# One list of weight loads across the stages of a decoder step, and modulation matmuls in groups of four

## The chip, the cores and the metric

The kernel runs on one core of a Trainium2 chip. The metric is the device time of one launch in microseconds (us), the median of several runs. A core has five engines with instruction queues of their own: TensorE (PE, with its weight loads as PEld), VectorE (DVE), ScalarE (ACT), GpSimd (POOL) and SyncE (SP), which here only issues DMA transfers. [...]

## What is computed

One inference step of a 2-layer decoder for 512 prompt tokens and 8 x 4 sample tokens (width 1024, all float32). Each layer has a mixer and a convolutional feed-forward net (FFN), both between RMS norms and modulated by shift, scale and gate, which come from a matmul of the condition `c` with `ada_w`:

```python
mod = (c_act @ w["ada_w"][l] + w["ada_b"][l])[:, None, :]
sh1, sc1, g1, sh2, sc2, g2 = jnp.split(mod, 6, axis=-1)
h = _rmsnorm(x, ng[0]) * (1 + sc1) + sh1
...
x = x + g1 * _rmsnorm(y, ng[1])
h = _rmsnorm(x, ng[2]) * (1 + sc2) + sh2
y, f_new = _conv_ffn(h, f_prev, w["ffn_w_up"][l], w["ffn_conv_w"][l], w["ffn_conv_b"][l], w["ffn_w_down"][l])
x = x + g2 * _rmsnorm(y, ng[3])
```

Mixer 0 is a gated convolution beside causal pooling, mixer 1 is dilated attention (the sample tokens against a cache) beside a convolution module. Outputs are the activations, the new convolution states and the shifted caches (`o_c`, copied from DRAM to DRAM).

## The kernel before

Tokens lie along the columns: 544 columns in two halves `h` of 272, features on the 128 partitions. A large matmul is done in three passes for accuracy: `Hhi*whi`, `Hlo*whi`, `Hhi*wlo` (lines 527, 529, 531). So every weight tile of 128 x 512 is loaded by SP into `wraw` (7 buffers), copied by ACT to the rounded `whi` (L510), and the remainder `wlo` is formed by DVE or POOL (L511); `whi` and `wlo` have 8 buffers each, which is four blocks of two tiles. A block of 128 outputs is 8 k-steps x 3 passes x 2 halves = 48 matmuls, and its result is evicted from PSUM by the stage's own function.

`gemm` (L536) runs one matmul of the model over its blocks. The first blocks of a stage (`lead`) and the last (`tail`) are done half by half, so that the norm of one half can run while TensorE works on the other; `junction` (L496: `postres`, then `premod`) is that norm. `gemm` loads a block's weights when it comes to the block; the lead's `wlo` are formed on POOL (30 tiles in all), the others on DVE. The stages are mixer 0 (`w_abi`, `w_abo`), FFN 0, mixer 1 (`w_cdi`, attention, `w_cdo`) and FFN 1.

Side work is woven in, one step after each block: `ada` (L397) for the modulation, `bias_vectors`, `caches`. One step of `ada` is four loads of 128 x 512 and four matmuls whose stationary operand has 32 columns, each to its own 32 partitions of one PSUM bank (128*32 in the profile); 8 steps make one third of a layer's modulation, then four transposes and a few DVE operations turn it to the partitions. The first of these is done at the start, before the first block, since nothing can begin without it; the five others run in mixer 0 and FFN 0.

A scheduler places the instructions on each engine's queue by its own estimate of when they can run; the order in the code is only where it starts. So the four matmuls of a step need not stand together, and a cache copy may stand far ahead of its place in the code.

Of the kernel before, what the change touches and what calls it, by code (L numbers as in the profile page):

```python
# [41 lines left out]
XRB = 6  # L42
# [225 lines left out]
def build(nc, tc, ctx, t):  # L268
# [21 lines left out]
    cst = cp.tile([P, NCST], F32, name="cst")  # L290
    cact = cp.tile([P, KB, 32], F32, name="cact")
# [97 lines left out]
    apool = []  # L389
# [7 lines left out]
    def ada(l, s):  # L397
        ps = psum1("psada")
        for k in range(KB):
            for j in range(4):  # L400
                wt = ada_tile()
                o = s * 2048 + j * 512
                SY.dma_start(wt, t["ada_w"][l, k, :, o:o + 512])
                PE.matmul(ps[32 * j:32 * j + 32, :], cact[:, k, :], wt, start=(k == 0), stop=(k == KB - 1))  # L404
            yield
        ev = np_.tile([P, 512], F32, name="adaev", tag="nsq", bufs=NSQ)
        A.activation(ev, ps, AF.Copy)
        pt = psum1("psadat")
# [42 lines left out]
    LEADE = G  # L451
# [52 lines left out]
    def load_w(ap, kc, eng):  # L504
        raw = wp.tile([P, 512], F32, name="wraw", tag="wraw", bufs=WRAW)
        hi = wp.tile([P, 512], F32R, name="whi", tag="whi", bufs=WSLOTS)
        lo = wp.tile([P, 512], F32R, name="wlo", tag="wlo", bufs=WSLOTS)
        n = kc * P
        SY.dma_start(raw[:, :n], ap.rearrange("p k n -> p (k n)"))
        A.activation(hi[:, :n], raw[:, :n], AF.Copy)  # L510
        eng.tensor_tensor(lo[:, :n], raw[:, :n], hi[:, :n], op=SUB)  # L511
        return hi, lo

    def load_block(w, n, k0, k1, eng):
        out = []
        for a in range(k0, k1, 4):
            b = min(a + 4, k1)
            hi, lo = load_w(w[n, :, a:b, :], b - a, eng[a // 4 % 2])
            out += [(hi[:, i * P:(i + 1) * P], lo[:, i * P:(i + 1) * P]) for i in range(b - a)]
        return out  # L520

    def mm(ps, wt, src, h0, h1):
        last = len(wt) - 1
        for i, (whi, wlo) in enumerate(wt):
# [5 lines left out]
            for h in range(h0, h1):  # L530
                PE.matmul(ps[:, h, :HT], wlo, xhi[:, h, :], start=False, stop=(i == last))  # L531
# [4 lines left out]
    def gemm(w, blocks, k0, k1, src, evac, lead=0, tail=0, mids=(None, None), eng=None, loaded=()):  # L536

        nb = len(blocks)

        def halves(idx, eng, mid):  # L540
            wts = dict(enumerate(loaded)) if 0 in idx else {}
            for h in range(2):
                for i in idx:
                    if h == 0 and i not in wts:
                        wts[i] = load_block(w, blocks[i], k0, k1, eng)
# [5 lines left out]
                    mm(ps, wts[i], src, h, h + 1)  # L551
                    evac(i, blocks[i], ps, h, h + 1)
# [4 lines left out]
        yield from halves(range(lead), (G, LEADE), mids[0])  # L557
# [5 lines left out]
        yield from halves(range(nb - tail, nb), (V, V), mids[1])  # L563
# [54 lines left out]
    def ffn(l, nxt, side, pre):  # L618
# [11 lines left out]
        if l == 0:  # L630
            apool.append((fp, 4))
# [42 lines left out]
        def body():  # L674
# [19 lines left out]
    def mixer0(nxt, side, pre, loaded):  # L694
# [5 lines left out]
        apool.append((st0, XRB))  # L700
# [587 lines left out]
```

## Time and profile before

| | us |
|---|---|
| median of 3 runs | 1503.35 (1501.24 to 1504.15) |
| the profiled execution | 1496.03 |
| its span | 1494.3 |
| PE busy | 1417.8 |
| DVE busy | 882.1 |
| ACT busy | 618.8 |
| POOL busy | 170.6 |

PE is busy for 95% of the span, and 88% of the chain that ended last is PE. A busy PE counts modelled ends of pipelined matmuls, so what a piece of work costs is read from the starts of the instructions around it. Of the rest of the span, most lies at the start, at the passages from one stage to the next (the junctions), in the second half of attention, and at the end.

### The profile page before, as it was taken

How to read it: one execution, taken by the hardware profiler on the slowest of the kernel's cores; microseconds unless marked ns; L12 is line 12 of the kernel's file. 1: busy time of each engine (PE TensorE's matmuls, PEld its weight loads, DVE VectorE, ACT ScalarE, POOL GpSimd, SP SyncE). 2: the span in 40 equal slices, each digit the busy share in tenths (PEclk: the TensorE clock that was granted, in tenths of full speed). 3: DMA queues.
4: the chain of work that ended last, by engine and by line, in shares of the span. 5: the costliest groups of instructions: out<-in, count | busy, mean ns of one | idle time of the engine just before them, and what ended most of it. 6: DMA issues, size and time to landing. Idle time of an engine off the chain costs nothing.

```text
span 1494.3 us, 26853 instructions
## 1 busy us (share of the span) xinstructions
PE 1417.8 (95%) x10354; PEld 1271.0 (85%) x10354; DVE 882.1 (59%) x1788; ACT 618.8 (41%) x1145; POOL 170.6 (11%) x384
## 2 busy tenths in 40 slices
PE   6899997999999999999799999999699999999995
PEld 2578897988798798899699999678599999999995
DVE  1664427753165346446859979652886456456457
ACT  2322235743244234235652442643674444244244
POOL 0210014110011001001500000000521011011011
PEclk9799998999999999999999999999899999999998
DMA  7775633325445546544236245446122332332311
GB/s 264 242 253 187 201 106 100 103 98 180 160 155 194 161 139 212 165 158 186 89 113 197 94 141 178 135 146 239 57 85 69 103 93 71 104 91 65 113 51 61
DMA packets 112633, 207.72 MB, mean 139 GB/s; under 512 B 20884, under 2 KB 33684, under 8 KB 111992
## 3 DMA queue, kind: packets, MB, share of 16 engines
q1 hardware_dynamic: 112504, 206.00, 42.5%
q8 instruction: 81, 1.33, 0.4%
q14 instruction: 48, 0.39, 0.1%
HBM read 198.63 MB, written 34.39 MB: 156 GB/s over the span
## 4 chain that ended last, share of the span: by engine, by line
PE 88%; DVE 6%; DMA 2%; ACT 2%; issue 1%; SPq 0%; POOL 0%; POOLq 0%; DVEq 0%; ACTq 0%
PE psmm L527 23%; PE psmm L531 23%; PE psmm L529 23%; PE psada L404 6%; PE psn L442 2%; PE psmh L529 2%; PE psmh L527 2%; PE psmh L531 2%; PE pso L1013 1%; PE psl L979 1%; PE psl L981 1%; DVE X L492 1%; DVE Yf L491 1%; DVE Y L491 1%; DVE Hlo L481 1%
## 5 line engine op out<-in xcount | busy, mean ns | idle before, releaser
L510 ACT ACTIVATE whi<-wraw 128x512 fp32r<-128x512 f32 (+1 forms) x404 | 239.8, 600 | 511.4 <-PE psmm L529 411.6
L527 PE MATMUL psmm<-Hhi,whi 128*128 128x272 f32 x2028 | 435.9, 291 | 1.0 <-DVE extu L750 1.0
L531 PE MATMUL psmm<-Hhi,wlo 128*128 128x272 f32 x2028 | 431.4, 289 | 0.3 <-POOL wlo L511 0.3
L529 PE MATMUL psmm<-Hlo,whi 128*128 128x272 f32 x2028 | 430.0, 288 | 0.0
L511 DVE TENSOR_TENSOR wlo<-wraw,whi 128x512 fp32r<-128x512 f32 (+1 forms) x374 | 240.8, 649 | 303.4 <-ACT whi L510 288.3
L527 PEld LDWEIGHTS psmm<-Hhi,whi 128*128 128x128 f32 x2028 | 321.4, 189 | 24.3 <-issue 12.6
L529 PEld LDWEIGHTS psmm<-Hlo,whi 128*128 128x128 f32 x2028 | 322.5, 189 | 9.0 <-issue 9.0
L531 PEld LDWEIGHTS psmm<-Hhi,wlo 128*128 128x128 f32 x2028 | 321.5, 189 | 9.9 <-issue 9.2
L527 PE MATMUL psmm<-act_hi,whi 128*128 128x272 f32 x624 | 135.5, 290 | 0.0
L531 PE MATMUL psmm<-act_hi,wlo 128*128 128x272 f32 x624 | 135.3, 289 | 0.0
L529 PE MATMUL psmm<-act_lo,whi 128*128 128x272 f32 x624 | 132.7, 288 | 0.0
L578 DVE SCALAR_TENSOR_TENSOR fz<-fext,par,fz 128x560 f32<-128x560 f32 x88 | 70.5, 801 | 74.3 <-ACT fz L577 74.2
L404 PE MATMUL psada<-adaw,cact 128*32 128x512 f32 x384 | 102.6, 628 | 8.3 <-DMA adaw<-ada_w 8.3
L527 PEld LDWEIGHTS psmm<-act_hi,whi 128*128 128x128 f32 x624 | 99.6, 188 | 11.8 <-issue 8.4
L531 PEld LDWEIGHTS psmm<-act_hi,wlo 128*128 128x128 f32 x624 | 99.6, 188 | 7.6 <-issue 7.5
L529 PEld LDWEIGHTS psmm<-act_lo,whi 128*128 128x128 f32 x624 | 99.1, 188 | 0.8 <-issue 0.8
L577 ACT ACTIVATE fz<-fext,par 128x560 f32<-128x560 f32 x88 | 75.2, 855 | 34.5 <-DVE fext L647 34.5
L874 DVE SCALAR_TENSOR_TENSOR zd<-extd,par,zd 128x512 f32<-128x512 f32 x120 | 87.0, 746 | 0.7
L569 POOL COPY fso<-fext 128x2 f32<-128x2 f32 x88 | 23.1, 263 | 530.6 <-ACT fext L646 530.6
L579 DVE SCALAR_TENSOR_TENSOR fz<-fext,par,fz 128x560 f32<-128x560 f32 x88 | 70.5, 801 | 2.7
L646 ACT ACTIVATE fext<-psmm 128x512 f32<-128x512 f32 (+1 forms) x88 | 49.7, 564 | 51.1 <-PE psmm L531 51.1
L527 PE MATMUL psmh<-Hhi,whi 128*128 128x272 f32 x148 | 48.2, 326 | 16.1 <-ACT Hhi L479 14.5
(260 smaller groups left out, 1692.9 us busy)
## 6 DMA issues: line engine op xcount, KB each, us to landing
adaw<-ada_w SPq DMA_DIRECT2D x192, 256.0 KB, 3.6
wraw<-w_up SPq DMA_DIRECT2D x176, 256.0 KB, 3.0
wraw<-w_dn SPq DMA_DIRECT2D x64, 256.0 KB, 2.8
o_c<-cache SPq DMA_DIRECT2D x8, 2040.0 KB, 10.0
wraw<-w_cdi SPq DMA_DIRECT2D x52, 256.0 KB, 4.6
wraw<-w_abi SPq DMA_DIRECT2D x32, 256.0 KB, 4.5
o_c<-cache SPq DMA_DIRECT2D x8, 1016.0 KB, 7.1
kc<-kc SPq DMA_DIRECT2D x28, 256.0 KB, 3.7
```

The lines of the kernel that those rows point to most:

```text
L404: PE.matmul(ps[32 * j:32 * j + 32, :], cact[:, k, :], wt, start=(k == 0), stop=(k == KB - 1))
L442: PE.matmul(ps, ones, a, start=(i == 0), stop=(i == n - 1))
L510: A.activation(hi[:, :n], raw[:, :n], AF.Copy)
L511: eng.tensor_tensor(lo[:, :n], raw[:, :n], hi[:, :n], op=SUB)
L527: PE.matmul(ps[:, h, :HT], whi, xhi[:, h, :], start=(i == 0), stop=False)
L529: PE.matmul(ps[:, h, :HT], whi, xlo[:, h, :], start=False, stop=False)
L531: PE.matmul(ps[:, h, :HT], wlo, xhi[:, h, :], start=False, stop=(i == last))
L577: A.activation(z[:, :n], ext[:, 2:2 + n], AF.Identity, bias=b, scale=w[:, 2:3])
L578: V.scalar_tensor_tensor(z[:, :n], ext[:, 1:1 + n], w[:, 1:2], z[:, :n], op0=M, op1=ADD)
L579: V.scalar_tensor_tensor(z[:, :n], ext[:, 0:n], w[:, 0:1], z[:, :n], op0=M, op1=ADD)
L646: A.activation(fpr(ext, 2, h0, h1), cpr(ps, h0, h1), AF.Copy)
L874: V.scalar_tensor_tensor(cpr(z), ip, dw[:, i:i + 1], cpr(z), op0=M, op1=ADD)
```

## The change

All weight loads of the launch are put in one list ahead of time (`declare`). `take` gives a block its weights, and before that issues the loads and splits of all blocks up to two ahead, across the ends of stages too; both splits are now on ACT and DVE, none on POOL. Evictions are placed behind the newest splits on ACT and on DVE (`evacuate`). `ada` loads two 128 x 512 pieces in one transfer of 512 KB and does four matmuls of 256 columns with it, placed right behind the newest block on PE, with nothing between the four; the six thirds become twelve halves of 8 steps. The turn to the partitions is two matmuls by a selection of 9 of each 32 columns in place of four transposes. Small and large output transfers (`queued`) are placed behind the newest weight load on SP, the cache copies one to every fourth block of FFN 1; those of `o_kv` and `rvd` go to ACT's queue. At the start, the norm of half 0 begins with the first half of the modulation.

```diff
     def ada_tile():
-        if apool:
-            ap, n = apool[-1]
-            return ap.tile([P, CH, HT], F32, name="adaw", bufs=n).rearrange("p a n -> p (a n)")[:, 0:512]
-        return wp.tile([P, 512], F32, name="adaw", tag="wraw", bufs=WRAW)
+        return apool[-1].tile([P, 2, 512], F32, name="adaw", bufs=ADB[len(apool) - 1])
...
+            with tc.issue_after(newest["PE"]) if "PE" in newest else nullcontext():
+                for j in range(4):
+                    PE.matmul(ps[32 * j:32 * j + 32, :], cact[:, k, :], wt[:, j // 2, 256 * (j % 2):256 * (j % 2) + 256],
+                              start=(k == 0), stop=(k == KB - 1))
...
-        for c in range(4):
-            PE.transpose(pt[:, c * P:(c + 1) * P], ev[:, c * P:(c + 1) * P], ident)
+            for c in range(2):
+                PE.matmul(pt[:, :, c, :], ev[:, c * P:c * P + P], ssel, start=True, stop=True)
...
-    def load_w(ap, kc, eng):
+    def load_w(ap):
...
-        eng.tensor_tensor(lo[:, :n], raw[:, :n], hi[:, :n], op=SUB)
...
+        newest["SP"] = SY.dma_start(raw[:, :n], ap).ins
+        newest["ACT"] = A.activation(hi[:, :n], raw[:, :n], AF.Copy).ins
+        newest["DVE"] = V.tensor_tensor(lo[:, :n], raw[:, :n], hi[:, :n], op=SUB).ins
...
+    def take():
+
+        u, i = done
+        need = max(units[u])
+        while i < len(loads) and (i <= need or i < WSLOTS or loads[i - WSLOTS][1] <= u - 2):
+            loads[i][2] = load_w(loads[i][0])
+            i += 1
+        done[:] = [u + 1, i]
+        return [x for j in units[u] for x in loads[j][2]]
+
+    def evacuate(evac, *args):
+
+        with tc.issue_after(newest["ACT"]), tc.issue_after(newest["DVE"]):
+            evac(*args)
...
-            mm(ps, load_block(w, blocks[i], k0, k1, eng or (V, V)), src, 0, 2)
-            evac(i, blocks[i], ps, 0, 2)
+            mm(ps, take(), src, 0, 2)
+            evacuate(evac, i, blocks[i], ps, 0, 2)
...
-                SY.dma_start(t[f"o_c{g}"][b:b + n].rearrange("b w n -> b (w n)").rearrange("b (q n) -> q b n", q=16),
-                             t[f"cache{g}"][b:b + n, 4:CW[g]].rearrange("b w n -> b (w n)").rearrange("b (q n) -> q b n", q=16))
+                with queued():
+                    SY.dma_start(t[f"o_c{g}"][b:b + n].rearrange("b w n -> b (w n)").rearrange("b (q n) -> q b n", q=16),
+                                 t[f"cache{g}"][b:b + n, 4:CW[g]].rearrange("b w n -> b (w n)").rearrange("b (q n) -> q b n", q=16))
...
-    pre = mixer0((0, 1), chain(delay(1), pace(chain(ada(0, 1), ada(0, 2)), 7, 8)),
-                 second, loaded)
-    pre = ffn(0, (1, 0), chain(delay(8), bias_vectors(), slow(chain(ada(1, 0), ada(1, 1), ada(1, 2)), 2)), pre)
+    pre = mixer0((0, 1), chain(delay(1), ada([(0, i, q) for i in (1, 2) for q in range(2)], 2, 0)),
+                 lambda: (xprep(1), first(1, 0, KB)))
+    pre = ffn(0, (1, 0), chain(delay(8), bias_vectors(), pace(ada([(1, i, q) for i in range(3) for q in range(2)], 1, 0), 3, 4)), pre)
     pre = mixer1((1, 1), pre)
-    ffn(1, None, caches(), pre)()
+    ffn(1, None, slow(caches(), 3), pre)()
```

On PE in FFN 0, before, where the first step of layer 1's modulation runs (`psada` is the modulation's PSUM bank, `psmm` a block's):

```order
L529 MATMUL psmm<-Hlo,whi 128x272 x2
L404 MATMUL psada<-adaw,cact 32x512 x2
L531 MATMUL psmm<-Hhi,wlo 128x272 x2
L527 MATMUL psmm<-Hhi,whi 128x272 x2
L529 MATMUL psmm<-Hlo,whi 128x272
L404 MATMUL psada<-adaw,cact 32x512
L529 MATMUL psmm<-Hlo,whi 128x272
L531 MATMUL psmm<-Hhi,wlo 128x272 x2
L527 MATMUL psmm<-Hhi,whi 128x272 x2
L529 MATMUL psmm<-Hlo,whi 128x272
L404 MATMUL psada<-adaw,cact 32x512
```

The same place after:

```order
L608 MATMUL psmm<-Hhi,whi 128x272 x2
L610 MATMUL psmm<-Hlo,whi 128x272 x2
L612 MATMUL psmm<-Hhi,wlo 128x272 x2
L431 MATMUL psada<-adaw,cact 32x256 x4
L608 MATMUL psmm<-Hhi,whi 128x272 x2
```

The step that stood in three places of a block stands in one, at the block's end. In the whole program before, `psada` stands in 84 places, 9 of them ahead of the first block; after, in 72, 5 of them ahead of it, and of the other 67, 54 hold four matmuls and 13 hold eight.

On DVE at the junction from mixer 1 to FFN 1, before (L446 to L448 end the norm's root, L491 and L492 are `postres`):

```order
L446 SCALAR_TENSOR_TENSOR nq<-nr 128x272
L596 TENSOR_TENSOR Y_10483<-psmh,Y_10483 128x272
L447 SCALAR_TENSOR_TENSOR nq<-psn,nq 128x272
L596 TENSOR_TENSOR Y_10483<-psmm,Y_10483 128x272
L448 SCALAR_TENSOR_TENSOR nr<-nq,nr 128x272
L596 TENSOR_TENSOR Y_10483<-psmh,Y_10483 128x272
L491 TENSOR_TENSOR Y_10483<-Y_10483,nr 128x2x272 x2
L492 TENSOR_TENSOR X<-X,Y_10483 128x2x272 x2
```

The same place after:

```order
L558 TENSOR_TENSOR wlo<-wraw,whi 128x512
L494 SCALAR_TENSOR_TENSOR nq<-nr 128x272
L676 TENSOR_TENSOR Y_10539<-psmm,Y_10539 128x272
L495 SCALAR_TENSOR_TENSOR nq<-psn,nq 128x272
L558 TENSOR_TENSOR wlo<-wraw,whi 128x512
L496 SCALAR_TENSOR_TENSOR nr<-nq,nr 128x272
L676 TENSOR_TENSOR Y_10539<-psmh,Y_10539 128x272
L538 TENSOR_TENSOR Y_10539<-Y_10539,nr 128x2x272 x2
L539 TENSOR_TENSOR X<-X,Y_10539 128x2x272 x2
```

The eight splits of FFN 1's lead, which stood in one row on POOL, now stand on DVE in and around this chain: three ahead of L538, three between L539 and the next root (behind L518), two around that root.

On SP, before, a cache copy stands among the weight loads of mixer 0:

```order
L509 DMA wraw<-w_abi 128x512 x4
L1207 DMA o_c<-cache 16x3968
L403 DMA adaw<-ada_w 128x512 x4
L509 DMA wraw<-w_abi 128x512 x3
L1207 DMA o_c<-cache 16x3968
```

After, all 24 stand in FFN 1:

```order
L556 DMA wraw<-w_up 128x512 x4
L1298 DMA o_c<-cache 16x16256
L556 DMA wraw<-w_up 128x512 x6
L1298 DMA o_c<-cache 32x16320
L556 DMA wraw<-w_up 128x512 x6
```

They moved from mixer 0, FFN 0 and mixer 1 into the stage that has no modulation to load.

## Rows read from the trace of the kernel before

**Rows 1.** Busy time by stretch of the span: start and end, length, busy us and instructions of PE, PEld, DVE, ACT and POOL, then TensorE's granted clock, the DMA engines' share and GB/s. The stretches are mixer 0, FFN 0, its junction to mixer 1, the second half of attention, the junction to FFN 1, and FFN 1.
```profile
60.00:228.00 168.00, 166.92 (x1203) 139.79 (x1203) 74.67 (x159) 48.46 (x86) 13.25 (x23) 1.00 0.58 188
258.00:697.00 439.00, 439.00 (x3208) 386.41 (x3207) 223.91 (x433) 169.81 (x288) 35.96 (x128) 1.00 0.47 157
697.00:757.00 60.00, 47.03 (x312) 43.34 (x311) 49.38 (x115) 39.42 (x100) 22.76 (x26) 0.94 0.38 136
950.00:1005.00 55.00, 48.99 (x357) 35.79 (x356) 34.78 (x77) 29.31 (x44) 0.00 (x0) 0.97 0.50 166
1050.00:1095.00 45.00, 30.44 (x165) 26.12 (x165) 38.65 (x83) 29.11 (x73) 18.45 (x15) 0.85 0.15 47
1095.00:1458.00 363.00, 363.00 (x2911) 362.72 (x2910) 212.11 (x401) 160.20 (x261) 43.21 (x128) 1.00 0.29 87
```

**Rows 2.** The same view with the instructions of the tile `psada` alone, from the first block to the end of the modulation: busy PE, PEld and ACT.
```profile
60.00:645.00 585.00, 79.34 (x320) 11.06 (x320) 2.97 (x5) 0.99 0.51 166
```

**Rows 3.** PE in order of time: start, length, line, result and operands, shapes, count of records (one of these float32 matmuls of the modulation leaves two records). First a step in three pieces, then a step in one.
```profile
332.47 0.29 PE L529 MATMUL psmm<-Hlo,whi 128*128 128x272 f32 x1
332.68 1.04 PE L404 MATMUL psada<-adaw,cact 128*32 128x512 f32 x2
333.66 0.40 PE L529 MATMUL psmm<-Hlo,whi 128*128 128x272 f32 x1
...
356.36 0.41 PE L531 MATMUL psmm<-Hhi,wlo 128*128 128x272 f32 x2
356.70 1.06 PE L404 MATMUL psada<-adaw,cact 128*32 128x512 f32 x8
357.69 0.52 PE L527 MATMUL psmm<-act_hi,whi 128*128 128x272 f32 x2
```

**Rows 4.** PE in order of time in mixer 1's last matmul, where the sample's attention does groups of four matmuls of the same form with 256 columns.
```profile
1024.08 0.41 PE L531 MATMUL psmm<-Hhi,wlo 128*128 128x272 f32 x2
1024.42 1.07 PE L1157 MATMUL psr<-vc,sPT 128*32 128x256 f32 x16
1025.42 0.52 PE L527 MATMUL psmm<-Hhi,whi 128*128 128x272 f32 x2
...
1026.03 0.41 PE L531 MATMUL psmm<-Hhi,wlo 128*128 128x272 f32 x2
1026.37 0.64 PE L1157 MATMUL psr<-vc,sPT 128*32 128x256 f32 x8
1026.94 0.52 PE L527 MATMUL psmm<-Hhi,whi 128*128 128x272 f32 x2
```

**Rows 5.** PE in order of time: the four transposes that turn a third of the modulation, and four float32 matmuls with 16 columns and a whole stationary operand.
```profile
417.58 0.60 PE L410 MATMUL psadat<-cst,adaev 128*128 128x128 f32 x4
417.94 0.49 PE L527 MATMUL psmm<-Hhi,whi 128*128 128x272 f32 x2
...
1035.82 0.96 PE L1168 MATMUL psys<-cst,Rm 128*128 128x16 f32 x8
1036.62 0.50 PE L527 MATMUL psmm<-Hhi,whi 128*128 128x272 f32 x2
```

**Rows 6.** The start: busy time by stretch, columns as in rows 1, then PE in order of time.
```profile
8.00:23.00 15.00, 11.19 (x35) 3.64 (x32) 0.59 (x2) 3.44 (x7) 0.00 (x0) 1.00 1.06 378
23.00:33.00 10.00, 9.28 (x38) 3.55 (x38) 4.84 (x10) 2.01 (x4) 0.00 (x0) 1.00 0.37 115
33.00:47.50 14.50, 8.25 (x22) 1.97 (x22) 2.69 (x12) 2.79 (x5) 3.60 (x7) 0.76 0.93 319
...
37.97 6.54 PE L404 MATMUL psada<-adaw,cact 128*32 128x512 f32 x16 [1.81 <-DMA adaw<-ada_w]
47.54 0.36 PE L527 MATMUL psmh<-Hhi,whi 128*128 128x272 f32 x1 [1.62 <-DVE Hhi L1238]
```

**Rows 7.** The junction from mixer 1 to FFN 1 in order of time: POOL, then DVE. The last two rows of DVE are half 1 of the same junction.
```profile
1048.95 12.24 POOL L511 TENSOR_TENSOR wlo<-wraw,whi 128x512 fp32r<-128x512 f32 x8 [11.17 <-PE psmm L531]
1053.51 3.13 DVE L491 TENSOR_TENSOR Y<-Y,nr 128x544 f32<-128x544 f32 x2
1056.57 3.49 DVE L492 TENSOR_TENSOR X<-X,Y 128x544 f32<-128x544 f32 x2
1059.98 2.42 DVE L491 TENSOR_TENSOR Y<-Y,nr 128x544 f32<-128x544 f32 x2
1081.15 1.36 DVE L491 TENSOR_TENSOR Y<-Y,nr 128x544 f32<-128x544 f32 x2
1082.43 1.35 DVE L492 TENSOR_TENSOR X<-X,Y 128x544 f32<-128x544 f32 x2
```

**Rows 8.** Groups of instructions by line and form: the `wlo` splits of whole tiles on DVE and on POOL; busy us, mean ns of one, and what ended the idle time ahead of them.
```profile
L511 DVE TENSOR_TENSOR wlo<-wraw,whi 128x512 fp32r<-128x512 f32 x318 | 217.3, 689 | 245.7 <-ACT whi L510 236.8 <-DMA wraw<-w_up 4.0 <-PE psadat L410 2.8
L511 POOL TENSOR_TENSOR wlo<-wraw,whi 128x512 fp32r<-128x512 f32 x30 | 43.9, 1482 | 82.8 <-ACT whi L510 36.2 <-DMA wraw<-w_abi 35.5 <-PE psmm L531 11.2
```

**Rows 9.** One link of the chain that ended last, in attention's second half.
```profile
988.80 4.93 DMA wraw<-w_cdo
```

**Rows 10.** DMA issues: result and source, queue, count, KB each, median us from issue to landing.
```profile
o_c<-cache SPq DMA_DIRECT2D x8, 2040.0 KB, 10.0
o_c<-cache SPq DMA_DIRECT2D x8, 1016.0 KB, 7.1
vc<-vc SPq DMA_DIRECT2D x14, 512.0 KB, 6.9
```

More of the change, by code (lines that the diff above doesn't have):

```diff
@@ L1 @@
 import numpy as np
-from contextlib import ExitStack
+from contextlib import ExitStack, nullcontext
 import concourse.bass as bass
@@ new lines, in build, with queued, last, ada @@
+    ssel = cp.tile([P, 4, NMOD], F32, name="ssel")
+    apool = [st0]
+    newest = {}
+    def queued():
+        return tc.issue_after(newest["SP"]) if newest else nullcontext()
+    def last(eng):
+        return tc.issue_after(next(i for i in reversed(nc.cur_bb.bb.instructions) if i.engine == eng.engine))
+    def ada_tile():
+        return apool[-1].tile([P, 2, 512], F32, name="adaw", bufs=ADB[len(apool) - 1])
+    def ada(halves, per, ahead):
+        todo = [(l, s, q, k) for l, s, q in halves for k in range(KB)]
+        tiles = []
+        def load():
+            if todo[len(tiles):]:
+                l, s, q, k = todo[len(tiles)]
+                tiles.append(ada_tile())
+                with queued():
+                    SY.dma_start(tiles[-1], t["ada_w"][l].rearrange("k p (s a q n) -> s q k p a n", s=3, a=2, q=2)[s, q, k])
+        for _ in range(ahead):
+            load()
+        outs = []
+        for i, (l, s, q, k) in enumerate(todo):
+            load()
+            if k == 0:
+                ps = psum1("psada")[:, 0:256]
+            wt = tiles[i]
+            with tc.issue_after(newest["PE"]) if "PE" in newest else nullcontext():
+                for j in range(4):
+                    PE.matmul(ps[32 * j:32 * j + 32, :], cact[:, k, :], wt[:, j // 2, 256 * (j % 2):256 * (j % 2) + 256],
+                              start=(k == 0), stop=(k == KB - 1))
+            if i % per == per - 1:
+                yield
+                for o in list(outs):
+                    if next(o, 0) == 0:
+                        outs.remove(o)
+            if k == KB - 1:
+                outs.append(ada_out(l, s, q, ps))
+                if ahead:
+                    for _ in outs.pop():
+                        pass
+        while outs:
+            for o in list(outs):
+                if next(o, 0) == 0:
+                    outs.remove(o)
+            yield
@@ L530, in mm, with gemm, halves @@
             for h in range(h0, h1):
-                PE.matmul(ps[:, h, :HT], wlo, xhi[:, h, :], start=False, stop=(i == last))
+                x = PE.matmul(ps[:, h, :HT], wlo, xhi[:, h, :], start=False, stop=(i == last))
+        newest["PE"] = x.ins
     def srcH(k):
         return Hhi[:, k], Hlo[:, k]
-    def gemm(w, blocks, k0, k1, src, evac, lead=0, tail=0, mids=(None, None), eng=None, loaded=()):
+    def gemm(blocks, src, evac, lead=0, tail=0, mids=(None, None)):
+        blocks = list(blocks)
         nb = len(blocks)
-        def halves(idx, eng, mid):
-            wts = dict(enumerate(loaded)) if 0 in idx else {}
+        def halves(idx, mid):
             for h in range(2):
                 for i in idx:
-                    if h == 0 and i not in wts:
-                        wts[i] = load_block(w, blocks[i], k0, k1, eng)
                     if i % 5 in (1, 3):
@@ L555, in halves @@
                     mid()
-        yield from halves(range(lead), (G, LEADE), mids[0])
+        yield from halves(range(lead), mids[0])
         for i in range(lead, nb - tail):
             ps = psum("psmm")
-            mm(ps, load_block(w, blocks[i], k0, k1, eng or (V, V)), src, 0, 2)
-            evac(i, blocks[i], ps, 0, 2)
+            mm(ps, take(), src, 0, 2)
+            evacuate(evac, i, blocks[i], ps, 0, 2)
             yield
-        yield from halves(range(nb - tail, nb), (V, V), mids[1])
+        yield from halves(range(nb - tail, nb), mids[1])
     def fill_state(ext, L, st):
@@ L682, in body @@
                 yield from up(e + 1, FGROUPS[gi + 1][1])
-            SY.dma_start(t[f"o_f{l}"], so)
-            yield from down(ng - 1)
-            apool.clear()
+            for i, _ in enumerate(down(ng - 1)):
+                if i == 3:
+                    with queued():
+                        SY.dma_start(t[f"o_f{l}"], so)
+                yield
+            del apool[1:]
         weave(body(), side)
@@ L1180, in sample @@
             yield
-        weave(gemm(t["w_cdo"], range(KB), 2, 6, lambda k: srcH(k + 2), out_evac(Y, acc, None, True, False)), sample())
-        for _ in gemm(t["w_cdo"], range(KB), 0, 2, srcH, out_evac(Y, acc, cG[1][0], False, True), tail=KB,
+        weave(gemm(range(KB), lambda k: srcH(k + 2), out_evac(Y, acc, None, True, False)), sample())
+        for _ in gemm(range(KB), srcH, out_evac(Y, acc, cG[1][0], False, True), tail=KB,
                       mids=(None, lambda: junction(0, Y, acc, nxt))):
@@ L1248, in build @@
     SY.dma_start(cst[:, :io], t["cst"][:, :io])
+    steps(a, 2)
+    xstat(0)
     steps(a, 1)
-    xprep(0, 0, KB)
-    steps(a, 1)
-    xprep(1, 0, CH * (XRB - 4))
-    loaded = [load_block(t["w_abi"], ABI[i], 0, KB, (G, G)) for i in range(PRE)]
+    xstat(1)
+    xprep(0)
+    for i in range(2):
+        loads[i][2] = load_w(loads[i][0])
+    done[1] = 2
     for _ in a:
```

186 lines of the change are left out of this document (105 added, 81 removed).

## The prediction, made before the changed kernel ran

> **What bounds the kernel now.** I read the busy time by stretch first. In FFN 0 PE is busy 439.00 us of 439, in FFN 1 363.00 of 363, in mixer 0 166.92 of 168 [rows 1]. There nothing can shorten the launch but less work on PE, and a wait put on another engine costs nothing until PE feels it. PE has idle time at the junctions (12.97 us of 60 from FFN 0 to mixer 1, 14.56 of 45 from mixer 1 to FFN 1), in attention's second half (6.01 of 55) [rows 1], and at the start, where the first block begins at 47.54 [rows 6]. So I cost the change in two ways: by PE's time in the full stretches, and by what ends last in the others.
>
> **The modulation's matmuls.** Busy shares don't price an interruption of the stream, so I take starts. A lone matmul of 512 columns: from the block's matmul ahead of it at 332.47 to the one behind it at 333.66 is 1.19 us; two neighbouring matmuls of the block stand 0.125 apart (48 of 363.00 us over 2911 records, [rows 1]), so the interruption costs 1.07. Four of them together: from 356.36 to 357.69 is 1.33, and the two records ahead account for 0.25, which leaves 1.08 [rows 3]. An interruption costs the same whether it holds one matmul or four. Counted by the order, 75 interruptions lie behind the first block, 75 x 1.07 = 80.3; the busy time of the tile gives 79.34 [rows 2], so the count is sound.
>
> After, there are 67: 54 of four and 13 of eight, all with 256 columns. The trace has this very form, in the sample's attention: 32 columns of stationary operand and 256 moving columns. Eight records (four matmuls, as in the step of [rows 3]) cost 1026.94 - 1026.03 - 0.25 = 0.66, sixteen cost 1025.42 - 1024.08 - 0.25 = 1.09 [rows 4]. So 54 x 0.66 + 13 x 1.09 = 49.8, and **the grouping saves 30.5**. PE does the same products; what goes is the fixed part of each interruption. Bounds: if the steps cost what [rows 3] show for any count, 67 x 1.07 = 71.7 and the saving is 8.6; if FFN's steps cost 0.55 (half of 1.09), it is 36.4. I take 30.5 since form, columns and number of records are those of [rows 4].
>
> [...]
>
> **The turn to the partitions.** Five groups of four transposes cost 417.94 - 417.58 = 0.36 each [rows 5], 1.8 in all. Ten groups of two float32 matmuls with 36 columns take their place. The nearest row is four such with 16 columns, 1036.62 - 1035.82 = 0.80 [rows 5], so two are 0.40; with some more columns 0.45, or 4.5 in all: **+2.7**. Bounds: -1 (two records like transposes) and +3.
>
> **The start.** DMA moves 378 GB/s from 8 to 23 us, 115 from 23 to 33, 319 from there to 47.5 [rows 6], which is 5.7 + 1.2 + 4.6 = 11.4 MB. The sag is the point: the seven buffers that the modulation's loads share stay full in it. After, pieces of 512 KB have buffers of their own, and the norm of half 0 starts with half the modulation. At 378 GB/s 11.4 MB take 30.3 us in place of 39.5, which is 9 less; and the last group before the first block, 6.54 us at a clock that is mean 0.76 of full in that stretch, begins after the last load [rows 6] and gets half as long. Against this, DVE takes over six splits of 0.69 [rows 8] = 4.1 and the norm's products of half 1. I take **-8**, with -2 (no gain in transfer, the short tail only) and -13 (both gains whole) as bounds.
>
> **The junctions.** Of the 30 POOL splits of 1.48 [rows 8] 24 stand at three junctions. From 1048.95 to 1061.19 POOL splits, and DVE's products and sums of the norm are slow: 3.13 and 2.42 for two L491, 3.49 for two L492. In the same junction's second half, without POOL, they take 1.36 and 1.35 [rows 7]. So POOL costs DVE 1.77 + 1.06 + 2.14 = 5.0 on the way to PE's next matmul, 15 at three junctions if all are alike. After, DVE does eight splits of 0.69 [rows 8] = 5.5 at each, 16.6 in all. DVE is idle 6.35 of 45 us in the last junction and 10.62 of 60 in the one before [rows 1], much of it waits between the steps of the norm's root, where three or four of the eight stand by the order; I count half as hidden. -15 + 8.3, taken as **-6**. Bounds: -12 (nearly all hidden), and +17 if all 24 lie open and nothing is given back.
>
> **Attention's second half.** The wait for `w_cdo`, 4.93 us, is a link of the chain [rows 9]. The list now loads its first blocks two ahead, which no longer begins with the stage. PE is idle 6.01 there in all [rows 1], and what comes next is the attention's own softmax; I take **-2**, bounds -4 and 0.
>
> **The held evictions** I cost at nothing. A split for block u+2 needs a buffer that block u-2 has left, and its data; it stands two blocks, 2 x 48 x 0.125 = 12 us, ahead of its matmul. An eviction behind it waits only if the load is late, and then PE waits too once its PSUM buffers are full. The same holds for the modulation's loads that are queued on SP behind the weights, as long as DMA keeps ahead. That cover is what the rivals take away. `o_kv` and `rvd` on ACT's queue have PE-full stretches around them and cost 0.
>
> **Sum:** -30.5 + 2.7 - 8 - 6 - 2 = -43.8. The profiled execution of 1496.03 would become 1452; the median shown is 7.3 above it, 1503.35, and that is the base of the measure, so 1503.35 - 43.8 = **1460**.
>
> **Rivals.** *The transfers of mixer 0 end last.* A pair of modulation steps falls on each block there, 1 MB beside 0.5 MB of weights; a 512 KB piece lands in 6.9 us [rows 10], a block takes 6 us of PE, and the stage moves 188 GB/s at a share of 0.58 [rows 1]. If two pieces in flight don't keep up, PE waits at each group and mixer 0 keeps its length: its part of the saving, some 40 of 75 interruptions or 43 us against 18, is lost. -43.8 + 25 = -19, **1484**. Against it: at the start 378 GB/s flow at a share of 1.06 [rows 6], twice as much. Chance 0.08.
>
> *The splits on DVE take POOL's place as the wait.* All 24 lie on the junctions' chains and DVE is no faster without POOL: +17 in place of -6, so -43.8 + 23 = -21, **1483**. For it: DVE is busy 38.65 of 45 [rows 1]. Against it: 1.36 beside 3.13 [rows 7]. Chance 0.10.
>
> *The open loads of the modulation.* If the number of matmuls sets the time, 40 steps x 4 matmuls more with two loads each are 320 loads of 0.125 (362.72 over 2910, [rows 1]) = 40: **1500**. [...] Against it: [rows 4]. Chance 0.02.
>
> *The copies choke FFN 1 (slower).* The cache copies now run only there, where PE has no idle us; the large ones land in 10.0 and 7.1, 8 x 10.0 + 8 x 7.1 = 137 us [rows 10]. Loads queued behind one on SP come late, their splits hold up the evictions, and PE stops. The change turns slower when over 44 of the 137, a third, show on PE. If half do, 1503 - 44 + 69 = **1528**. Against it: 12 us of lead exceed the longest copy, and the stage uses 0.29 of the DMA engines [rows 1]. Chance 0.05.
>
> **How the numbers follow.** My forecast has 0.70, the rivals 0.08, 0.10, 0.02 and 0.05; the last 0.05 is for a larger gain, since start and junctions may give some 10 more. The forecast's own unknowns (start -2 to -13, junctions -12 to 0, grouping to -36) give 1445 to 1472; to leave out no more than 0.2 the range takes in the first two rivals: 1440 to 1485. A difference of 0.2%, 3 us, is about what a measurement of this kernel can tell from no change. Faster: 0.70 + 0.08 + 0.10 + 0.05 = 0.93; the same: the open loads, 0.02; slower: the copies, 0.05.
>
> **What would show it.** In the profile after, interruptions of 0.66 for eight records and 1.09 for sixteen, and `psada` at some 50 busy in place of 79.34, show the first term; the first block's first matmul near 39.5 the third; L491 at 1.4 for two in all junctions, and three junctions together some 6 shorter, the fourth. PE busy below 100% in FFN 1 with DMA as releaser would show the copies; idle PE ahead of `psada` in mixer 0 the transfers; a stream with full PE but 0.9 or more for a step, the open loads. I am wrong most likely where small idle times at many blocks add up, since FFN 0 and FFN 1 are 802 us of full PE and 1% of them is 8.

## The result, and the profile after

The changed kernel takes **1448.3 us** (median of 4, 1446.55 to 1448.82) against 1502.3 of the kernel before beside it (median of 4, 1496.79 to 1504.15): a ratio of **0.9644**, 95% interval 0.9617 to 0.9672. The forecast was 1460 in a range from 1440 to 1485. By the medians 54 us went, by the two profiled executions 47.5 (1496.03 to 1448.51). The profiled execution of before lies 6 us below the median of its runs, that of after on it, so some 6 us of the 54 are not to be found in these two traces.

Busy time by stretch, columns as in [rows 1]: mixer 0, FFN 0, its junction to mixer 1, the junction to FFN 1, FFN 1; last, the tile `psada` alone (PE, PEld, ACT), which answers to [rows 2].

```profile
56.00:222.00 166.00, 165.01 (x1377) 150.91 (x1376) 79.24 (x170) 53.26 (x105) 14.93 (x25) 1.00 0.51 168
260.00:640.00 380.00, 380.00 (x3101) 352.78 (x3100) 195.25 (x370) 142.76 (x240) 27.43 (x115) 1.00 0.44 142
643.00:720.00 77.00, 67.62 (x469) 60.40 (x461) 58.02 (x145) 49.80 (x123) 13.47 (x23) 0.96 0.33 99
999.00:1055.00 56.00, 45.93 (x279) 41.71 (x278) 51.03 (x130) 42.31 (x102) 10.93 (x15) 0.85 0.23 75
1055.00:1403.00 348.00, 348.00 (x2780) 348.00 (x2779) 194.27 (x369) 140.25 (x236) 32.00 (x119) 1.00 0.49 161
...
52.00:655.00 603.00, 48.42 (x640) 13.92 (x640) 3.33 (x9) 1.00 0.46 147
```

FFN 0 and FFN 1 are as full as before, FFN 1 with the copies' traffic in it (161 GB/s). `psada` has twice the records, 640, in 48.42 us.

PE in order of time, a step of four matmuls and two steps together (answers to [rows 3, 4]):

```profile
300.89 0.41 PE L612 MATMUL psmm<-Hhi,wlo 128*128 128x272 f32 x2
301.23 0.64 PE L431 MATMUL psada<-adaw,cact 128*32 128x256 f32 x8
301.80 0.52 PE L608 MATMUL psmm<-Hhi,whi 128*128 128x272 f32 x2
...
103.75 0.41 PE L612 MATMUL psmm<-Hhi,wlo 128*128 128x272 f32 x2
104.09 1.07 PE L431 MATMUL psada<-adaw,cact 128*32 128x256 f32 x16
105.09 0.52 PE L608 MATMUL psmm<-Hhi,whi 128*128 128x272 f32 x2
```

From start to start, less 0.25: 301.80 - 300.89 - 0.25 = 0.66, and 105.09 - 103.75 - 0.25 = 1.09, the two prices taken from the attention's groups.

The start, by stretch and on PE (answers to [rows 6]):

```profile
8.00:23.00 15.00, 9.01 (x57) 2.87 (x54) 0.00 (x0) 2.68 (x5) 0.00 (x0) 1.00 1.01 338
23.00:33.00 10.00, 9.38 (x60) 5.77 (x58) 4.43 (x14) 4.10 (x8) 0.00 (x0) 1.00 0.80 276
33.00:42.00 9.00, 5.08 (x46) 2.57 (x42) 8.87 (x26) 4.80 (x10) 1.36 (x5) 0.85 1.00 364
...
39.08 1.01 PE L431 MATMUL psada<-adaw,cact 128*32 128x256 f32 x8 [0.99 <-DMA adaw<-ada_w]
42.08 0.57 PE L608 MATMUL psmh<-Hhi,whi 128*128 128x272 f32 x1
```

The sag to 115 GB/s is gone (276), and between the last load's matmuls and the first block lie 3.0 us in place of 9.6.

The same matmul of the same block stands in both traces, so the difference can be put down to places. The next table compares starts of block matmuls at the stages' ends; the modulation's interruptions in each are summed from start to start.

| from the start of ... to ... | before | after | difference | of it modulation and turn | rest |
|---|---|---|---|---|---|
| the program to the tail of mixer 0's last matmul | 211.45 | 193.23 | -18.2 | -8.5 | -9.7 |
| that tail to FFN 0's first block behind the lead | 70.97 | 61.50 | -9.5 | 0 | -9.5 |
| FFN 0 to its tail | 410.11 | 388.67 | -21.4 | -22.1 | +0.7 |
| that tail to mixer 1's first block behind the lead | 75.78 | 76.56 | +0.8 | +2.4 | -1.6 |
| mixer 1 to its tail | 271.41 | 273.16 | +1.8 | 0 | +1.8 |
| that tail to FFN 1's first block behind the lead | 65.49 | 61.93 | -3.6 | 0 | -3.6 |
| FFN 1 from there to its last matmul | 372.21 | 375.27 | +3.1 | 0 | +3.1 |
| the end | 16.85 | 16.37 | -0.5 | 0 | -0.5 |

So the modulation gave some 28 (30 in its matmuls, 2 taken by the turn: ten groups at 0.36 to 0.44 each where five at 0.35 to 0.51 stood), the start 9.7, the junctions 14.7; some 5 were lost in mixer 1 and FFN 1. Of the start's 9.7, 5.5 lie ahead of the first block (47.54 to 42.08), the rest behind it in mixer 0.

The three junctions are not alike. Busy time in the first of them, in the kernel before, in the changed kernel, and in the kernel before with one edit (e12 below):

```profile
211.45:282.42 70.97, 62.96 (x423) 59.28 (x422) 48.88 (x107) 41.40 (x96) 23.49 (x29) 0.93 0.28 91
...
193.23:254.73 61.50, 58.94 (x423) 55.49 (x421) 46.31 (x115) 41.00 (x97) 11.04 (x21) 1.00 0.25 74
...
210.40:271.47 61.07, 59.04 (x422) 55.41 (x421) 42.84 (x110) 38.45 (x91) 7.90 (x19) 1.00 0.34 109
```

PE's idle time in it (length less busy) falls from 8.0 to 2.6 us, and the same 423 records take 4.0 us less, at a mean granted clock of 1.00 of full speed in place of 0.93. In the other two PE's idle time falls by 3.6 and 4.5, and nothing comes back from the clock (0.95 to 0.96, and 0.90 to 0.86).

### The profile page after: what moved, and what is told of

The parts are those of the page before. It is cut to its first block, busy times and chain, and to the rows that moved or that the text cites. A ratio compares the mean times of both kernels' runs of the same rounds, so it can differ in the third digit from the quotient of the medians.

```text
span 1446.7 us, 27425 instructions
## 1 busy us (share of the span) xinstructions
PE 1381.9 (96%) x10762; PEld 1280.2 (88%) x10762; DVE 874.0 (60%) x1833; ACT 609.2 (42%) x1151; POOL 118.1 (8%) x354
## 4 chain that ended last, share of the span: by engine, by line
PE 87%; DVE 7%; DMA 3%; ACT 2%; issue 1%; POOL 0%; SPq 0%; POOLq 0%; DVEq 0%; ACTq 0%
PE psmm L608 24%; PE psmm L610 23%; PE psmm L612 23%; PE psada L431 3%; PE psn L490 3%; PE psmh L608 2%; PE psmh L610 2%; PE psmh L612 1%; PE pso L1099 1%; PE psl L1065 1%; PE psl L1067 1%; DVE wlo L558 1%; DMA kc<-kc 1%; DMA X<-x 1%; DVE X L539 1%
## 5 line engine op out<-in xcount | busy, mean ns | idle before, releaser
L557 ACT ACTIVATE whi<-wraw 128x512 fp32r<-128x512 f32 (+1 forms) x404 | 233.7, 597 | 377.6 <-PE psmm L610 345.4
L558 DVE TENSOR_TENSOR wlo<-wraw,whi 128x512 fp32r<-128x512 f32 (+1 forms) x404 | 256.4, 650 | 200.8 <-ACT whi L557 192.8
L431 PE MATMUL psada<-adaw,cact 128*32 128x256 f32 x768 | 62.1, 411 | 12.4 <-DMA adaw<-ada_w 12.4
L727 DVE COPY fext<-psmm 128x32 f32<-128x32 f32 (+1 forms) x88 | 16.5, 187 | 90.7 <-ACT fext L726 89.5
```

The lines of the kernel that those rows point to most:

```text
L431: PE.matmul(ps[32 * j:32 * j + 32, :], cact[:, k, :], wt[:, j // 2, 256 * (j % 2):256 * (j % 2) + 256], start=(k == 0), stop=(k == KB - 1))
L557: newest["ACT"] = A.activation(hi[:, :n], raw[:, :n], AF.Copy).ins
L558: newest["DVE"] = V.tensor_tensor(lo[:, :n], raw[:, :n], hi[:, :n], op=SUB).ins
```

## The experiments

All times below are medians of 4 runs; beside them the kernel before on the same chip had 1502.4 (e1 to e4), 1498.7 (e5 to e8) and 1501.3 (e9 to e12).

| | us | ratio to the kernel before (95%) |
|---|---|---|
| the change | 1448.3 | 0.9644 (0.9617 to 0.9672) |
| e1 leads' splits on POOL | 1462.7 | 0.9743 (0.9719 to 0.9766) |
| e2 no loads across stages | 1446.4 | 0.9633 (0.9614 to 0.9652) |
| e3 modulation in pairs | 1488.3 | 0.9915 (0.989 to 0.994) |
| e4 two steps together in FFN 0 | 1441.8 | 0.9602 (0.9582 to 0.9621) |
| e5 idle work on POOL | 1472.6 | 0.9828 (0.9809 to 0.9847) |
| e6 evictions not held | 1520.6 | 1.0146 (1.0127 to 1.0165) |
| e7 copies not queued | 1454.0 | 0.9698 (0.9682 to 0.9715) |
| e8 e2 and e4 | 1440.3 | 0.9605 (0.9589 to 0.9622) |
| e9 e6 and e7 | 1466.2 | 0.9764 (0.975 to 0.9779) |
| e10 two buffers | 1459.1 | 0.9717 (0.9702 to 0.9732) |
| e11 one turn at the start | 1448.9 | 0.9648 (0.963 to 0.9666) |
| e12 before, leads' splits on DVE | 1483.7 | 0.988 (0.9863 to 0.9896) |

### The junctions: POOL, or the list?

```diff
 e1 (load_w, for the leads of FFN 0, mixer 1 and FFN 1)
+        if lead:
+            G.tensor_tensor(lo[:, :n], raw[:, :n], hi[:, :n], op=SUB)
+        else:
             newest["DVE"] = V.tensor_tensor(lo[:, :n], raw[:, :n], hi[:, :n], op=SUB).ins
 e2 (take; stage holds the first load of each stage)
-        while i < len(loads) and (i <= need or i < WSLOTS or loads[i - WSLOTS][1] <= u - 2):
+        while i < len(loads) and (i <= need or (i not in stage and (i < WSLOTS or loads[i - WSLOTS][1] <= u - 2))):
 e5 (load_w, for the same leads; idle is a scratch tile)
+            for i in range(0, n, P):
+                G.tensor_tensor(idle, raw[:, i:i + P], hi[:, i:i + P], op=SUB)
 e12 (the kernel before)
-        yield from halves(range(lead), (G, LEADE), mids[0])
+        yield from halves(range(lead), (V, V), mids[0])
```

> The changed kernel, with the 24 splits of the three later leads back on POOL (loads still listed ahead). After less before, by the starts of the same block matmuls, the three junctions are about 16 us shorter (9.5, 2.9 and 3.6). Theory A, POOL's splits slow DVE's norm work and that is the junctions' gain: 10 to 16 us of it are lost, L538 again takes 2.4 to 3.1 us for two beside POOL's splits and 1.36 without. Theory B, the gain comes from loads and splits issued before the stage ends: the time stays within 4 us, since they are still issued ahead.

> The changed kernel, with no load or split of FFN 0, mixer 1 or FFN 1 issued before the stage's own first block; splits still on DVE. Theory A (POOL off DVE's norm): within 4 us of the changed kernel. Theory B (loads ahead across the stages): 10 to 16 us slower, and the first matmul of each lead waits for its load or split.

> The changed kernel, its splits on DVE, and POOL forming the same 24 splits of the three leads once more, in quarters of 128 columns, into a scratch tile that nobody reads; DVE's, ACT's and PE's orders are the same. With the splits themselves on POOL the three junctions were 18.6 us longer (7.6, 5.6, 5.4). Theory A, POOL at work beside DVE slows DVE: 10 to 19 us slower than the changed kernel. Theory B, the loss there was the slow splits (1.48 against 0.69) that TensorE waited for: within 4 us of the changed kernel.

> The kernel before with one edit: the splits of the leads on DVE in place of POOL (28 of 30; two stay, those loaded ahead at the start). With POOL given idle work beside the changed kernel the three junctions were 23 us longer, with the splits themselves 18.6. Theory A, POOL at work beside DVE is the price, whatever the loading order: 12 to 20 us faster than the kernel before. Theory B, without loads ahead the lead's splits on DVE lie on the chain: within 4 us of the kernel before, or slower.

In e1 the three junctions are 7.6, 5.7 and 5.4 us longer than in the changed kernel, by the starts of the same matmuls; 14 us longer in all, since this execution's start was 3 shorter. In e2 the medians differ by 2 us, inside the intervals. In e12 the kernel before gains 17.6 by the medians with one edit, as theory A said. By the two traces it is 12.1 (the spans are 1494.3 and 1482.2): the junctions give 9.9, 4.4 and 3.0, but FFN 0 takes 3.7 more and mixer 1 2.0 more, which stays open. In e5, where the splits stay on DVE and nobody reads what POOL forms, the junctions are 6.5, 10.4 and 9.4 longer; the whole is 24 us slower, over theory A's 19.

The norm on DVE in mixer 1's junction to FFN 1, first half; the changed kernel:

```profile
1006.52 1.35 DVE L538 TENSOR_TENSOR Y<-Y,nr 128x544 f32<-128x544 f32 x2
1007.79 1.35 DVE L539 TENSOR_TENSOR X<-X,Y 128x544 f32<-128x544 f32 x2
1009.06 1.35 DVE L538 TENSOR_TENSOR Y<-Y,nr 128x544 f32<-128x544 f32 x2
```

e1, POOL and DVE:

```profile
1011.34 12.25 POOL L559 TENSOR_TENSOR wlo<-wraw,whi 128x512 fp32r<-128x512 f32 x8 [11.20 <-PE psmm L618]
...
1015.90 3.14 DVE L538 TENSOR_TENSOR Y<-Y,nr 128x544 f32<-128x544 f32 x2
1018.96 3.49 DVE L539 TENSOR_TENSOR X<-X,Y 128x544 f32<-128x544 f32 x2
1022.38 2.42 DVE L538 TENSOR_TENSOR Y<-Y,nr 128x544 f32<-128x544 f32 x2
```

e5, POOL and DVE (one line further down in the code):

```profile
1016.26 23.47 POOL L561 TENSOR_TENSOR idle<-wraw,whi 128x128 bf16<-128x128 f32 x32 [11.20 <-ACT whi L558]
...
1021.28 1.61 DVE L539 TENSOR_TENSOR Y<-Y,nr 128x544 f32<-128x544 f32 x2
1022.81 1.87 DVE L540 TENSOR_TENSOR X<-X,Y 128x544 f32<-128x544 f32 x2
1024.60 1.87 DVE L539 TENSOR_TENSOR Y<-Y,nr 128x544 f32<-128x544 f32 x2
...
1039.69 6.39 POOL L693 TENSOR_TENSOR yacc<-yacc,nsq 128x272 f32<-128x272 f32 x6
...
1040.48 0.43 ACT L691 ACTIVATE nsq<-Y 128x272 f32<-128x272 f32 x1 [7.81 <-POOL yacc L693]
```

Theory A stands as to place: the leads' splits on POOL are the price, with the list (e1) or without it (e12). How they cost is told by the rows. Beside POOL's splits, 12.25 / 8 = 1.53 us each, a DVE instruction takes 3.14 / 2 = 1.57 in place of 0.68; beside pieces of 23.47 / 32 = 0.73 it takes 0.81 to 0.94. In these rows it goes at about one DVE instruction per POOL instruction; by what the one holds up the other is not shown.

A second cause was left out of the theories: POOL does work of the norm itself (`yacc`, a part of its sum), and in POOL's queue that stands behind the splits. PE's wait in the first junction before, with POOL there in order of time:

```profile
PE psn L442 <- POOL yacc L606: 3.2, 1, 3.2
...
248.13 2.38 POOL L511 TENSOR_TENSOR wlo<-wraw,whi 128x512 fp32r<-128x512 f32 x1
250.47 1.49 POOL L606 TENSOR_TENSOR yacc<-yacc,nsq 128x272 f32<-128x272 f32 x1
```

In e1 this wait is back with the same 3.2; in the change and in e12 it is absent. And e5 is no clean test of the slower DVE: behind its idle work ACT waits 7.81 us for `yacc` in the junction to FFN 1, PE 5.7 in the one to mixer 1. How much of e5's 24 us is DVE's alone was not measured.

### The grouping

```diff
 e3 (ada; pend is run in the middle of the next block's matmuls)
-                for j in range(4):
-                    PE.matmul(ps[32 * j:32 * j + 32, :], cact[:, k, :], ...)
+            two((0, 1))
+                pend.append(two)
 e4
-... pace(ada([(1, i, q) for i in range(3) for q in range(2)], 1, 0), 3, 4) ...
+... pace(ada([(1, i, q) for i in range(3) for q in range(2)], 2, 0), 3, 8) ...
```

> The changed kernel, each modulation step's four matmuls given in two pairs, half a block apart; same matmuls, same loads. Theory A, an interruption costs 0.23 us plus 0.43 for each pass of 256 columns over the array, and up to four matmuls on different 32 columns share a pass: 84 pairs of 0.66, 28 groups of 1.09 and 6 of 0.66 are 89.9 against 50.1 us in the changed kernel, so 40 us slower. Theory B, time goes by the number of matmuls (0.165 each): no change.

> The changed kernel, with two modulation steps together (eight matmuls) at every second place in FFN 0 as in mixer 0; same loads. Theory A (0.23 for an interruption): 24 of 1.09 in place of 48 of 0.66, 5 us faster. Theory B (time by matmuls): no change. If three buffers of 512 KB are too few for two steps together, PE waits ahead of psada in FFN 0 and it is slower.

e3 is 40.0 us slower than the change, e4 6.5 faster (in FFN 0 to its tail 382.15 against 388.67), where theory A had 40 and 5. A pair in e3, PE in order of time:

```profile
310.01 0.41 PE L628 MATMUL psmm<-Hhi,wlo 128*128 128x272 f32 x2
310.35 0.63 PE L433 MATMUL psada<-adaw,cact 128*32 128x256 f32 x4
310.91 0.52 PE L624 MATMUL psmm<-Hhi,whi 128*128 128x272 f32 x2
```

Two matmuls cost 310.91 - 310.01 - 0.25 = 0.65, as four do. So theory A holds as far as was measured: a fixed 0.23, and 0.43 for every pass of 256 columns, the same for two matmuls as for four (0.66 and 1.09 give both prices; with 512 columns one matmul and four cost the same too, 1.07 and 1.08 [rows 3]).

### The evictions and the copies

```diff
 e6 (evacuate)
-        with tc.issue_after(newest["ACT"]), tc.issue_after(newest["DVE"]):
-            evac(*args)
+        evac(*args)
 e7 (caches); e9 has both edits
-                with queued():
+                with nullcontext():
                     SY.dma_start(t[f"o_c{g}"]...
```

> The changed kernel without the rule that evictions stand behind the newest splits on ACT and DVE. Theory A (the prediction's): the rule costs and gives nothing, within 3 us. Theory B, the rule costs the 3.3 us that the junction from FFN 0 to mixer 1 gave when loads were not issued ahead: 3 to 5 us faster. Theory C, the rule keeps weights early for TensorE in the full stages: slower, with idle PE in FFN 0 and FFN 1 and whi or wlo as releasers.

> The changed kernel with the cache copies not queued behind weight loads, so that they stand in mixer 0, FFN 0 and mixer 1 again. Theory A (the copies are hidden wherever they stand, since DMA keeps ahead): within 3 us. Theory B, copies in FFN 1 cost PE there: faster, in FFN 1's stretch. Theory C, copies beside the modulation's loads in mixer 0 make those late: slower, in mixer 0's stretch.

> The changed kernel with neither of two rules: evictions not held behind the splits, cache copies not queued behind the weight loads. Without the first alone FFN 1 was 75 us longer and FFN 0 the same; at 1153 us seven weight tiles had landed, DMA stood still to 1178, and ACT had evictions of two coming blocks queued ahead of the tiles' copies. Theory A, the scheduler's estimate puts the splits there because of the copies in the list, so without copies in FFN 1 the rule is worth nothing: FFN 1 is as in the changed kernel and the time within 5 us of 1454, that of the kernel with free copies. Theory B, the rule is needed in FFN 1 whatever stands on SP: over 1500.

e6 is 72 us slower than the change, all of it in FFN 1 (452.7 against 375.3 from the lead's end); FFN 0 is the same. So theory C holds for FFN 1 alone. FFN 1 by busy time, in the change and in e6; then, in e6, waits of PE there and of the loads on SP from 1140 to 1185 (total, times and longest); two stretches with the DMA share and GB/s last; and ACT in order of time:

```profile
1055.05:1430.32 375.27, 373.67 (x2980) 373.14 (x2978) 216.02 (x423) 155.09 (x269) 34.41 (x122) 1.00 0.46 152
...
1053.20:1505.91 452.71, 401.32 (x2961) 394.64 (x2959) 218.23 (x427) 158.86 (x274) 32.28 (x124) 0.92 0.37 126
...
PE psmm L607 <- ACT whi L557: 30.0, 9, 4.9
PE psmm L611 <- DVE wlo L558: 13.1, 14, 1.9
...
SPq L556 <- DVE wlo L558: 40.0, 8, 25.0
...
1155.00:1160.00 5.00, 5.00 (x42) 5.00 (x41) 1.60 (x2) 0.87 (x2) 0.20 (x1) 1.00 0.68 266
1160.00:1175.00 15.00, 11.36 (x92) 11.14 (x90) 7.38 (x14) 4.54 (x8) 1.54 (x8) 0.98 0.00 0
...
1171.45 0.60 ACT L725 ACTIVATE fext<-psmm 128x512 f32<-128x512 f32 x1 [4.13 <-PE psmm L611]
...
1175.58 3.21 ACT L557 ACTIVATE whi<-wraw 128x512 fp32r<-128x512 f32 x6
```

The tiles had landed by 1160, and DMA stood still for 15 us because their buffers were not emptied, as the loads' own waits for `wlo` say: ACT waited 4.13 us for a block's matmuls with six copies queued behind that eviction, and PE then waited for the copies. Without the hold the scheduler had put them there. The waits are not the whole of the 77 us that FFN 1 lost: PE's idle time rose from 1.6 to 51.4, some 50, and its busy time by 28, at a mean granted clock of 0.92 in place of 1.00. So over a third of the loss is busy time at the lower clock. Behind the wait for the six copies two block matmuls took 1176.86 - 1176.24 = 0.62 us in place of 0.25; what lowers the clock is not shown.

e7 lost 5.7 us, more than theory A allowed and where none of the three had it: its junction from FFN 0 to mixer 1 is 6.5 longer than in the change. PE, then DVE in order of time, then a stretch of e7 as above; last, PE's longest wait in the same junction of e9:

```profile
675.76 1.31 PE L490 MATMUL psn<-nsq,onesD 128*128 128x272 f32 x5
686.74 0.59 PE L608 MATMUL psmh<-act_hi,whi 128*128 128x272 f32 x1 [9.67 <-DVE Yf L676]
...
685.64 0.69 DVE L558 TENSOR_TENSOR wlo<-wraw,whi 128x512 fp32r<-128x512 f32 x1
686.25 0.43 DVE L676 TENSOR_TENSOR Yf<-psmh,Yf 128x272 f32<-128x272 f32 x1
...
660.00:685.00 25.00, 15.78 (x107) 13.21 (x105) 15.93 (x45) 13.28 (x34) 0.78 (x1) 0.92 0.04 12
...
PE psn L490 <- DVE Yf L687: 12.3, 1, 12.3
```

PE waits 9.67 us for an eviction (L676). It stands behind a split, and the split behind the whole norm of the next half, which DVE finishes at 685.6. From 660 to 685 hardly anything moved (12 GB/s), so it is again the order on DVE and not a late transfer. That the hold is to blame, by passing the split's late place on to the eviction, is not shown: e9 has no hold, and there the same junction is 5.2 longer than in the change, with one wait of 12.3 us of PE for DVE. What e7 and e9 share is the free copies.

e9 missed theory A's number (1466 against 1454) and confirmed its place: FFN 1 is as short as in the change (373.7 from the lead's end to its last matmul, 375.3 there), and FFN 0, where copies stand now, takes 405.75 to its tail in place of 388.67. The stall follows the copies. So the hold is worth 72 us with the copies in FFN 1 and 12 with the copies spread out, the lower clock included in both (a mean of 0.963 in e6 and 0.977 in e9, for 0.983 in the change and 0.981 in e7). That it is the scheduler's estimate of the copies which moves the splits is the reading that fits e6, e7 and e9; the estimate itself was not looked at.

### The start and mixer 0

```diff
 e10
-ADB = (4, 3)
+ADB = (2, 3)
 e11 (ada, at the start)
-                if ahead:
-                    for _ in outs.pop():
-                        pass
+                if ahead and i == len(todo) - 1:
+                    while outs:
+                        for _ in outs.pop(0):
+                            pass
```

> The changed kernel with two buffers of 512 KB in place of four for the modulation's pieces at the start and in mixer 0. The first rival of the prediction said that the pieces may end last in mixer 0; with two buffers a pair can only be asked for when the pair before is used. Theory A (transfers keep ahead of a block's 7.2 us even so, the pieces land in 4.3): mixer 0 after its lead stays 112 us, the start is some 2 to 6 us later for its loads. Theory B (buffers cover the transfers): a pair lands about 8 us after the block that frees its buffers ends, PE waits 1 to 8 us at each of 13 groups, 20 to 60 us slower.

> The changed kernel with the first third of the modulation turned to the partitions at once, when both halves are there, so that no chunk of the norm can begin with the first half; loads unchanged. The start (to the first block behind mixer 0's lead) was 11.2 us shorter than before without the grouping's part. Theory A, this comes from the loads alone: within 1.5 us. Theory B, the half-norm ahead carries part of it: four chunks of about 1.7 us on DVE come after the last load, 4 to 7 us slower.

e10's first block comes at 52.92 (42.08), and mixer 0 from its lead to its tail takes 112.9 (112.2). PE's waits up to 60 us from the start, the change and then e10:

```profile
PE psada L431 <- DMA adaw<-ada_w: 12.4, 10, 5.2
```

```profile
PE psada L431 <- DMA adaw<-ada_w: 19.8, 11, 5.6
```

So four buffers matter at the start, twice what theory A allowed (10.8 against 2 to 6; the waits are 7.4 of it, and the granted clock is 0.50 from 33 to 52 us in e10), and in mixer 0 two would do: the transfers keep ahead there. e11 is level with the change: the half-norm ahead carries nothing that can be measured, the start's gain is the loads'.

### Together

```diff
 e8: the edit of e2 and that of e4
```

> The changed kernel with the two edits that were faster together: no loads ahead across stages (-1.9 us by the medians) and modulation steps in twos in FFN 0 (-6.5). If they add up, 1439.9; the one works at the junctions and the other inside FFN 0, so no reason is seen why they should not.

e8 came to 1440.3, and its ratio is that of e4 alone. The junction from FFN 0 to mixer 1, 3.3 us shorter in e2 than in the change, is 0.6 shorter in e8, so e2's small gain is not established. Two steps together in FFN 0 is the edit that makes the changed kernel faster.

## Why the prediction held, and where it did not

**The modulation** was right in size: some -30 measured by starts for -30.5, the turn +2 for +2.7. The reason that the forecast names is wrong: "what goes is the fixed part of each interruption". By the 0.23 and 0.43 of e3 and e4 the fixed part is 8 places x 0.23 = 1.8 of it. Nearly all the rest is passes of 256 columns: two at each of the 75 places before, whether one matmul stood there or four, so 150, and 54 + 2 x 13 = 80 after. The size came out since both prices were read from rows and needed no reason. e3 shows the sharing of passes by undoing it (40 expected, 40.0 measured). The rival of the open loads is refuted by the 0.66 and by `psada`'s weight loads, 640 of them busy for 13.92 us in all. What the forecast did not see is that halving the columns was itself a loss: a step of 512 columns in one place cost 1.08, and the change does two places of 0.66; e4 takes 0.23 of each such pair back.

**The start**, -8 forecast, gave -9.7, from the loads and their buffers (e10), not from the half-norm (e11), which the forecast had counted on without a price of its own. The sign that it named missed: the first block came at 42.08 and not near 39.5, and 4.2 of the gain lie behind it.

**The junctions** are the term that was mis-sized: -6 forecast, -14.7 measured, -9.5, -1.6 and -3.6 one by one. The failing step is the price of POOL's work: 5.0 read in one half of one junction and taken as 15 "if all are alike". The second step, "I count half as hidden", 8.3 us open of the 24 splits on DVE, was nearer. The chain that ended last in the changed kernel holds splits for 2.5, 0.5 and 2.5 us at the three junctions, in the last these:

```profile
1002.45 0.60 DVE wlo L558
...
1003.56 0.69 DVE wlo L558
...
1005.30 0.60 DVE wlo L558
...
1017.22 0.60 DVE wlo L558
```

So at most 5.5 lie open, and the price of POOL was 14.7 to 20 (in e12, with 4.6 on the chain, 17.3 to 22). The surplus lies in the first junction, which gave 9.5 for a price of 5.0: 4.0 of it is the granted clock, which the forecast had at nothing, and 3.2 the wait for POOL's own `yacc`, which it did not look for. In the other two the gain is less than 5.0. The rival with all splits open (1483) is refuted.

**Attention's second half**, -2 forecast, gave nothing; mixer 1 became 1.8 longer. The link of `w_cdo` in the chain [rows 9] fell from 4.93 to 2.59, but PE's waits for the cache's transfers (`kc`) in attention rose from 2.6 to 4.2: the forecast had looked for what comes next in the softmax only.

**The held evictions** at nothing were right as a cost and misread as a part: without the hold the rest of the change would have been slower than the kernel before (1.0146, e6). The list and the copies in FFN 1 need it. The slower rival saw the right danger (copies, then splits, then evictions) by the wrong cause: in e6 and e7 the tiles had landed in time, and what was late was their copies' and splits' place in an engine's order.

**The transfers of mixer 0** are refuted even with half the buffers (e10). This rival was also priced too high: 25 of the interruptions stand in mixer 0, not some 40 of 75, so 9 us were at stake and not 25. FFN 1 lost 3.1 us: 1.35 in its tail, and not in the kernels with free copies (e7 and e9: 25.2 against 26.5), so the copies cost that; 1.7 between the lead and there (347.0 to 348.7), in neighbouring block matmuls 0.1253 apart on average where they had been 0.1246. e7 has the 348.7 too, e12 the 347.0, and in mixer 1 the distance grew from 0.1246 to 0.1255, most of its 1.8. Why stays open. So do the 6 us by which the medians differ more than the profiled executions.

**The sum** came near in the traces (-47.5 for -43.8) partly by luck: the junctions gave 8.7 more than forecast, and 5 of that went again in mixer 1 and FFN 1, which the forecast had at -2 and 0.

## What to carry to other kernels

Price a small interruption of TensorE's stream by the starts around it: here a fixed 0.23 us paid per place, and 0.43 for a pass of 256 columns that two or four matmuls shared (0.65 and 0.66); then put as many in a place as the buffers allow. Work moved to an idle POOL was not free here, with DVE on the chain beside it (1.57 us for an instruction of 0.68) and a later step of the chain behind it in POOL's own queue (a wait of 3.2). Where a wait of PE goes, look at the granted clock too: here 4.0 us came back at one junction where it was 1.00 in place of 0.93, and 28 us of busy time were added at 0.92 in e6. In an engine's queue look at what stands behind a waiting eviction before anything else: the same weights, landed in time, cost 72 us for standing behind it (ACT's wait of 4.13 held up six copies), and over a third of FFN 1's loss there was busy time at the lower clock.

## What the runs showed that was not expected

Beside POOL, a DVE instruction of 0.68 us took about as long as POOL's own (1.57 beside 1.53, 0.81 to 0.94 beside 0.73). Two matmuls of the modulation cost as much as four (0.65 and 0.66). In e6 DMA stood still for 15 us (0 GB/s) while PE waited for weights, and that meant not late transfers but full buffers: the loads waited 40.0 us for `wlo`.
